# First buffer filled in two loads split by partitions, and the first block's store queued behind the last loads

## The chip, the cores and the metric

One core of a Trainium2 chip. Times are device microseconds (us) of an execution; most executions of one kernel agree within 0.3%. Runs that were repeated are compared in the fast state only.

## The reference, cut to what matters

```
x: 32 x 512 x 1024 float32, random          # 16,384 rows of 1024, 67 MB
return np.sum(x, axis=-1)                   # 16,384 sums
```

## The kernel before

128 partitions hold the rows. A first block gives 112 rows to each partition, a second block 16. A buffer `xt` is 16 rows a partition: 64 KiB in each of 128 partitions, 8 MiB. Three buffers rotate; SyncE issues the loads, VectorE adds up the rows; ScalarE helps with the last two buffers. The very last buffer comes in pieces.

```
while c < whole:
    m = min(G, whole - c)                                    # G = 16 rows
    xt = xpool.tile([P, G * D], F32, tag="xt", name="xt")    # 3 buffers
    parts = (0, 1, m) if done + c == 0 else (0, m)           # first buffer: 1 row, then 15
    for i, k in zip(parts, parts[1:]):
        nc.sync.dma_start(out=xt[:, i * D : k * D], in_=x_b[:, (c + i) * D : (c + k) * D])
    ...                                                      # reductions on VectorE, some on ScalarE
if not final:
    for i, k in ((0, 104), (104, P)):
        nc.scalar.dma_start(out=out_b[i:k], in_=res[i:k])    # first block's sums, 448 B a partition
...                                                          # last loads, in five pieces
store = nc.sync.dma_start(out=out_b, in_=res)                # second block's sums
```

The first two loads are moved ahead of the start-up barrier by a pass over the compiled program, in both kernels.

Of the kernel before, what the change touches and what calls it, by code (L numbers as in the profile page):

```python
# [1 line left out]

# [4 lines left out]

F32 = mybir.dt.float32
ADD = mybir.AluOpType.add
COPY = mybir.ActivationFunctionType.Copy  # L10
X = mybir.AxisListType.X

BLOCKS = (112, 16)
G = 16
ACT_ROWS = 7
CUT = 544
EARLY = 2


@with_exitstack  # L20
def row_sums(
    ctx: ExitStack,
    tc: tile.TileContext,
    x: bass.AP,
    out: bass.AP,
):
    nc = tc.nc
    P = nc.NUM_PARTITIONS

    x_flat = x.flatten_outer_dims()  # L30
    R, D = x_flat.shape
    C = R // P
    assert R % P == 0 and sum(BLOCKS) == C
    out_flat = out.rearrange("a (b c) -> (a b c)", c=1)

    xpool = ctx.enter_context(tc.tile_pool(name="x", bufs=3))
    rpool = ctx.enter_context(tc.tile_pool(name="res", bufs=1))


    tail = rpool.tile([P, D + 16], F32, name="tail")  # L40
    part = tail[:, CUT + 14 : CUT + 15]
    nc.vector.memset(tail[:, CUT + 15 : CUT + 16], 0.0)  # L42
    seen = rpool.tile([P, 2], F32, name="seen")
    pairs = [rpool.tile([P, D // 2], F32, name=f"pairs{i}") for i in range(3)]

    def rows_dve(xt, res, j, n, c):
        nc.vector.tensor_reduce(  # L47
            out=res[:, c : c + n],
            in_=xt[:, j * D : (j + n) * D].rearrange("p (j d) -> p j d", d=D),
            axis=X,  # L50
            op=ADD,
        )

    def sum_act(v, acc):
        return nc.scalar.activation(out=v, in_=v, func=COPY, accum_out=acc)  # L55

    by_act = []

    def rows_act(xt, res, j, n, c):
        for i in range(n):  # L60
            by_act.append(
                sum_act(xt[:, (j + i) * D : (j + i + 1) * D], res[:, c + i : c + i + 1])
            )

    def pairs_dve(v, a, b, acc, pairs):
        h = (a + b) // 2
        nc.vector.tensor_tensor_reduce(  # L67
            out=pairs[:, 0 : h - a], in0=v[:, a:h], in1=v[:, h:b], scale=1.0, scalar=0.0,
            op0=ADD, op1=ADD, accum_out=acc,
        )  # L70

    def block(r0, n):
        x_b = x_flat[r0 : r0 + P * n].rearrange("(p c) d -> p (c d)", p=P)
        out_b = out_flat[r0 : r0 + P * n].rearrange("(p c) -> p c", p=P)
        return x_b, out_b, rpool.tile([P, n], F32, name=f"res{r0}")

    full = C - G
    done = 0
    for b, n in enumerate(BLOCKS):
        x_b, out_b, res = block(done * P, n)  # L80
        final = b == len(BLOCKS) - 1
        whole = n - G if final else n
        c = 0
        while c < whole:
            m = min(G, whole - c)
            xt = xpool.tile([P, G * D], F32, tag="xt", name="xt")
            parts = (0, 1, m) if done + c == 0 else (0, m)
            for i, k in zip(parts, parts[1:]):
                nc.sync.dma_start(
                    out=xt[:, i * D : k * D], in_=x_b[:, (c + i) * D : (c + k) * D]  # L90
                )
            a = ACT_ROWS if done + c + m == full else 0
            rows_dve(xt, res, 0, m - a, c)
            rows_act(xt, res, m - a, a, c + m - a)
            c += m
        if not final:

            for i, k in ((0, 104), (104, P)):
                nc.scalar.dma_start(out=out_b[i:k], in_=res[i:k])
        done += n  # L100

    xt = xpool.tile([P, G * D], F32, tag="xt", name="xt")
    cuts = [0, 9, 13, 15]
    for i, k in zip(cuts, cuts[1:]):
        nc.sync.dma_start(out=xt[:, i * D : k * D], in_=x_b[:, (c + i) * D : (c + k) * D])  # L105
    last = 15 * D
    for i, k, gap in ((0, CUT, 0), (CUT, D, 16)):
        nc.sync.dma_start(
            out=tail[:, i + gap : k + gap],
            in_=x_b[:, c * D + last + i : c * D + last + k],  # L110
        )

    by_act.clear()
    for i, k in zip(cuts[:2], cuts[1:3]):
        h = (k - i) // 2
        rows_dve(xt, res, i, h, c + i)
        rows_act(xt, res, i + h, k - i - h, c + i + h)
    pairs_dve(xt, 13 * D, 14 * D, res[:, c + 13 : c + 14], pairs[2])
    rows_act(xt, res, 14, 1, c + 14)
    pairs_dve(tail, 0, CUT, part, pairs[0])  # L120


    nc.vector.tensor_copy(out=seen, in_=tail[:, CUT + 14 : CUT + 16])  # L123
    pairs_dve(tail, CUT + 14, D + 16, res[:, c + 15 : c + 16], pairs[1])


    tc.keep_in_program_order(nc.sync.keepalive_nop([nc.sync.lower_ap(res[:, c + 14 : c + 15])]))
    store = nc.sync.dma_start(out=out_b, in_=res)
    for i in by_act:
        tc.declare_no_dep(store.ins, i.ins, reason="the wait is in the nop before it")  # L130


def kernel(tc: tile.TileContext, x: bass.AP, out: bass.AP):
    row_sums(tc, x, out)
    tc.close()
    tc.compile()  # L136



    sp = mybir.EngineType.SP  # L140
    fn = tc.nc.m.functions[0]
    entry, body = None, None
    for blk in fn.blocks:
        ops = [i for i in blk.instructions if i.engine == sp]
        if entry is None:
            entry = blk
        elif any(i.opcode == "DMACopy" for i in ops):
            body = blk
            break
    code = list(body.instructions)  # L150
    loads = [i for i in code if i.engine == sp][:EARLY]
    for load in loads:
        assert load.opcode == "DMACopy" and not load.sync_info.on_wait
        code.remove(load)
    body.instructions = code
    code = list(entry.instructions)
    at = next(k for k, i in enumerate(code) if i.engine == sp and i.opcode == "Drain")
    code[at:at] = loads
    entry.instructions = code

# [1 line left out]
_INS = ['x']  # L162
_OUTS = [((32, 512), 'float32')]


# [23 lines left out]
```

## Time and profile before

| | before |
|---|---|
| time, median | 162.14 us (162.09 to 162.2, 3 runs) |
| span in the profile | 160.4 us |
| time from one buffer's reduction to the next | 19.35 us |
| VectorE for one buffer | 17.22 us |
| start of the first reduction | 21.84 us |

The page of the kernel before, its parts 1 and 2: busy time by engine, then what the DMA engines moved in each of 40 equal slices of the span (4.0 us each).

```profile
span 160.4 us, 122 instructions
DVE 121.4 (76%) x17; ACT 17.2 (11%) x31; POOL 0.2 (0%) x4
...
GB/s 376 490 368 368 490 523 261 523 523 261 523 523 261 523 523 261 523 523 261 523 507 278 523 490 294 523 474 310 523 425 359 523 392 392 441 395 369 431 393 79
```

The slices swing between 261 and 523 only because a packet of 64 KiB is counted whole where it starts (16 of them in a slice of 4.01 us make 261 GB/s, 32 make 523). Averaged over three slices the rate is some 435 GB/s (523, 261 and 523 make 436) from shortly after the start to near the end. With VectorE waiting for every buffer, the loads have no slack: a microsecond that the DMA engines lose at the start should be a microsecond at the end.

### The profile page before, as it was taken

Reading aid. Unit: us, or ns where it says so; the run is one execution under the profiler, and the core shown is the slowest. Engines: PE = TensorE matmul, PEld = TensorE weight load, DVE = VectorE, ACT = ScalarE, POOL = GpSimd, SP = SyncE. Lnnn points to the kernel's source line nnn. Section 1 sums busy time; section 2 is a strip of 40 time slices with the busy share of each in tenths; the row PEclk is TensorE's granted clock in tenths of the full one; section 3 lists DMA queues with packets and bytes.
Section 4 is the critical chain, followed back from the end, with each engine's and each line's share of the span. In section 5 each row is a group of like instructions: output and inputs, shape, how many; then the busy total and the mean of one; then the engine's idle time right before and its main releaser. Section 6 shows DMA issues by size and latency. Waiting matters only on the chain.

```text
span 160.4 us, 122 instructions
## 1 busy us (share of the span) xinstructions
DVE 121.4 (76%) x17; ACT 17.2 (11%) x31; POOL 0.2 (0%) x4
## 2 busy tenths in 40 slices
DVE  0000059997799959999499994999949998698883
ACT  0000000000000000000000000000000000695892
POOL 0000000000000000000000000000000000000000
DMA  9988996996996996996996996997998999998992
GB/s 376 490 368 368 490 523 261 523 523 261 523 523 261 523 523 261 523 523 261 523 507 278 523 490 294 523 474 310 523 425 359 523 392 392 441 395 369 431 393 79
DMA packets 2169, 67.18 MB, mean 419 GB/s; under 512 B 505, under 2 KB 633, under 8 KB 889
## 3 DMA queue, kind: packets, MB, share of 16 engines
q1 hardware_dynamic: 2016, 67.12, 97.4%
q10 hardware_dynamic: 153, 0.06, 0.1%
HBM read 67.11 MB, written 0.07 MB: 419 GB/s over the span
## 4 chain that ended last, share of the span: by engine, by line
DMA 75%; DVE 22%; SPq 0%; issue 0%; DVEq 0%
DMA xt<-in_x_dram 75%; DVE res L47 21%; DVE pairs L67 1%; SPq L105 0%; DVE seen L123 0%; DVE tail L67 0%; DVEq L136 0%; DVE res L67 0%
## 5 line engine op out<-in xcount | busy, mean ns | idle before, releaser
L47 DVE TENSOR_REDUCE res<-xt 128x16 f32<-128x16384 f32 (+3 forms) x9 | 119.8, 13308 | 35.1 <-DMA xt<-in_x_dram 35.1
L55 ACT ACT_TABLE_LOAD x1 | 1.3, 1283 | 137.9 <-DMA xt<-in_x_dram 137.9
L55 ACT ACTIVATE xt<-xt 128x1024 f32<-128x1024 f32 x15 | 15.6, 1043 | 2.5 <-DMA xt<-in_x_dram 2.5
L55 ACT ACTIVATION_READ_ACCUMULATOR xt<-xt 128x1 f32 x15 | 2.8, 186 | 0.0
L42 DVE MEMSET tail<- 128x1 f32 x1 | 0.1, 59 | 1.3 <-PEq L173 1.3
L67 DVE CUSTOM_DVE_ANT_0 pairs<-xt 128x512 f32<-128x512 f32 x1 | 0.7, 692 | 0.3 <-DMA xt<-in_x_dram 0.3
L67 DVE CUSTOM_DVE_ANT_0 pairs<-tail 128x272 f32<-128x272 f32 (+1 forms) x2 | 0.9, 426 | 0.0
L123 DVE COPY seen<-tail 128x2 f32<-128x2 f32 x1 | 0.2, 168 | 0.0
L67 DVE DVE_READ_ACCUMULATOR2_ANT res<- 128x1 f32 x2 | 0.2, 82 | 0.0
L173 POOL MEMSET const-bfloat16-1.0<- 128x1 bf16 x1 | 0.1, 103 | 0.0
L173 POOL MEMSET const-uint8-127<- 128x1 uint8 x1 | 0.1, 102 | 0.0
L173 POOL MEMSET const-float32-1.0<- 128x1 f32 x1 | 0.1, 100 | 0.0
L173 POOL MEMSET const-float32-0.0<- 128x1 f32 x1 | 0.1, 99 | 0.2 <-issue 0.2
L67 DVE DVE_READ_ACCUMULATOR2_ANT tail<- 128x1 f32 x1 | 0.1, 80 | 0.0
## 6 DMA issues: line engine op xcount, KB each, us to landing
xt<-in_x_dram SPq DMA_DIRECT2D x1, 7680.0 KB
xt<-in_x_dram SPq DMA_DIRECT2D x1, 4608.0 KB, 32.6
xt<-in_x_dram SPq DMA_DIRECT2D x1, 2048.0 KB, 37.1
xt<-in_x_dram SPq DMA_DIRECT2D x1, 1024.0 KB, 39.2
xt<-in_x_dram SPq DMA_DIRECT2D x1, 512.0 KB, 3.6
tail<-in_x_dram SPq DMA_DIRECT2D x1, 272.0 KB, 39.3
tail<-in_x_dram SPq DMA_DIRECT2D x1, 240.0 KB, 39.2
xt<-in_x_dram SPq DMA_DIRECT2D x6, 40.8
```

Source lines behind the costliest of these rows:

```text
L42: nc.vector.memset(tail[:, CUT + 15 : CUT + 16], 0.0)
L47: nc.vector.tensor_reduce(out=res[:, c : c + n], in_=xt[:, j * D : (j + n) * D].rearrange("p (j d) -> p j d", d=D), axis=X, op=ADD,)
L55: return nc.scalar.activation(out=v, in_=v, func=COPY, accum_out=acc)
L67: nc.vector.tensor_tensor_reduce(out=pairs[:, 0 : h - a], in0=v[:, a:h], in1=v[:, h:b], scale=1.0, scalar=0.0, op0=ADD, op1=ADD, accum_out ...
L123: nc.vector.tensor_copy(out=seen, in_=tail[:, CUT + 14 : CUT + 16])
L173: nc = _bacc.Bacc("TRN2", target_bir_lowering=False, num_devices=1)
```

## The change

Its intent, as far as the code shows it: let the first load be short in descriptors (16 rows of 64 KiB, one for each DMA engine) so that bytes flow early, and keep the first block's store out of the way of the last loads.

```diff
-            parts = (0, 1, m) if done + c == 0 else (0, m)
+            parts = (0, 16, P) if done + c == 0 else (0, P)
             for i, k in zip(parts, parts[1:]):
-                nc.sync.dma_start(
-                    out=xt[:, i * D : k * D], in_=x_b[:, (c + i) * D : (c + k) * D]
-                )
+                nc.sync.dma_start(out=xt[i:k, 0 : m * D], in_=x_b[i:k, c * D : (c + m) * D])
...
         if not final:
-            for i, k in ((0, 104), (104, P)):
-                nc.scalar.dma_start(out=out_b[i:k], in_=res[i:k])
+            out_a, res_a = out_b, res
...                                   # behind the last loads:
+    for i, k in ((0, 64), (64, P)):
+        nc.sync.dma_start(out=out_a[i:k], in_=res_a[i:k])
```

## The prediction

> **What bounds the kernel now.** I read the page first, then the order of time near the start and at the end, then the records of single DMA packets in the trace. Part 3 of the page comes first, because this kernel reads 67 MB and computes little:
>
> ```profile
> DMA packets 2169, 67.18 MB, mean 419 GB/s; under 512 B 505, under 2 KB 633, under 8 KB 889
> ## 3 DMA queue, kind: packets, MB, share of 16 engines
> q1 hardware_dynamic: 2016, 67.12, 97.4%
> q10 hardware_dynamic: 153, 0.06, 0.1%
> ```
>
> The queue of loads keeps all 16 DMA engines busy for 97.4% of the span; hardly anything is left to fill. VectorE, the next busiest, is at 76%. The order of time shows the same from the consumer's side:
>
> ```profile
> 99.18 17.22 DVE L47 TENSOR_REDUCE res<-xt 128x16 f32<-128x16384 f32 x1 [2.14 <-DMA xt<-in_x_dram]
> ...
> 118.53 17.22 DVE L47 TENSOR_REDUCE res<-xt 128x16 f32<-128x16384 f32 x1 [2.13 <-DMA xt<-in_x_dram]
> ...
> 137.88 9.75 DVE L47 TENSOR_REDUCE res<-xt 128x9 f32<-128x9216 f32 x1 [2.13 <-DMA xt<-in_x_dram]
> ```
>
> One 8 MiB buffer arrives every 19.35 us (118.53 - 99.18; again 137.88 - 118.53), 8,388,608 B / 19.35 us = 433.5 GB/s, and VectorE needs 17.22 us for it and then stands idle for 2.13 us until the next lands. Eight such periods are 154.8 us of the 160.4 us span. The chain of waits names VectorE for 21.5%, but only because it follows a buffer's release back to a reduction: the six plain full loads take 40.8 us from issue to landing, two periods, so each stands behind a whole load already queued, and a reduction that ends a little earlier or later changes nothing.
>
> The end, and the store that is moved:
>
> ```profile
> 147.72 0.99 ACTq L99 DMA_DIRECT2D out_dram<-res  x2
> ...
> 156.52 0.69 DVE L67 CUSTOM_DVE_ANT_0 pairs<-xt 128x512 f32<-128x512 f32 x1 [0.28 <-DMA xt<-in_x_dram]
> ...
> 158.18 0.35 SPq L128 DMA_DIRECT2D out_dram<-res  x1
> ```
>
> The first block's store goes out at 147.72 us, 9 us ahead of the last loads; after these land, 1.66 us of VectorE work and the final store remain.
>
> In the packet records, a full load is 128 packets of 65,536 B, 8 on each DMA engine, each taking 2.418 us, that is 27.1 GB/s an engine, one after the other without gaps. The first packets start 1.01 us into the span; after the eight 4,096 B rows of the first load the engines begin their second load between 2.72 and 3.28 us, and this spread stays.
>
> [...]
>
> **The change part by part.** First the small parts.
>
> *The store.* Removed from the middle of the last loads: on one engine up to 8 + 2 packets of 448 B at 25 ns and two semaphore packets of 9 ns, some 0.27 us. They are put behind the last load, 8 packets an engine, 0.2 us, between the last load's packets (157.2 us) and the final store's (159.03 us), so hidden. SyncE has nothing else to do from 118.9 to 157.7 us, so its wait for the first block's results (ready at 147.6 us) holds up no load. Worth: -0.25 us.
>
> *The start.* One packet of 64 KiB on each engine in place of eight of 4 KiB. Eight rows at 0.159 us are 1.27 us, yet the slowest engine took 3.28 - 1.01 = 2.27 us. If long packets ramp without that loss, up to -0.5 us, less than the 1.0 us because the same late starts of engines stay. Descriptors and bytes are otherwise nearly the same in number.
>
> *The first 16 partitions.* 16 rows of 64 KiB, one an engine[...] four rows take 4 x 2.418 = 9.67 us[...]. Unhindered it would be 2.418 us. **Cost: +7.25 us**, on the path, because [...]the queue never has a gap in which to catch up.
>
> *The other 112 partitions.* Seven rows an engine. I take it [...]that the rows are dealt in runs of seven consecutive partitions, engine e getting 16 + 7e and up. [...]
>
> *Sum*, if the ports bind: 162.14 + 7.25 + (5 to 9.7) - 0.75 = 174 to 178 us. Everything after the first buffer shifts as a whole: the next reduction is still released by a load, the next loads are still issued a load ahead, and 19.35 us a buffer cannot be shortened.
>
> **The rivals.** *A: ports do not bind.* Each engine is the limit at 27.1 GB/s and any partition is as good as another. Then 1 + 7 rows are 8 rows as before, and only the small parts remain: 161.4 us. For it: whoever writes such a first split presumably saw it do no harm[...].[...]
>
> *B: only the first load suffers.* [...]just +7 to +10 us is left: 169 to 172 us.
>
> *C: the store becomes the bound.* SyncE sleeps on the first block's results and the final store is late. Against it: those results are there 10 us before the last load lands, and nothing but the nop and the final store follows. Worth at most 0.5 us.
>
> *D: VectorE catches up.* It is idle 2.13 us a buffer, but it has nothing to work on until a load lands, so it recovers none of a late load. Rejected.
>
> **Range and chances.** I give the port mechanism about two in three: [...]nothing in the trace shows it. Within it I expect 168 to 180 us with most weight at 172 to 178; without it 161.4, at most 1 us either way. Prediction 174 us, range 161 to 180 us, which covers both worlds; beyond it lies unfair sharing of ports. Slower by over 2% (above 165.4 us) 0.66; within 2% 0.33; faster by over 2% (under 158.9) 0.01, as 97.4% busy engines leave no such gain.
>
> **What would show it right or wrong.** If right, the first reduction starts near 38 us rather than 21.84, the first 65,536 B packets take about 9.7 us each instead of 2.4, later buffers keep 19.35 us, and the share of busy DMA engines stays high although GB/s is low in the first tenth of the span. If rival A is right, the first reduction starts near 21.5 us with packets of 2.4 us. If B, near 30 us. For the store: semaphore packets of q10 gone, q1 at 160 packets more than the loads' own change, and the last load to the end of the span as before, some 3.2 us from the last reduction's first part. What would make the sum wrong: another dealing of the 112 rows over engines[...].

Its sum came to 174 to 178 us: 162.14, + 7.25 for the first 16 partitions, + 5 to 9.7 for the other 112, - 0.75 for the store and the start. The 7.25 is 3 x 2.418 us; that four rows get the rate of one engine between them was an assumption then, which p1 bears out below (8.8 us a packet). "Port" is whatever engines share that write partitions of one group; the probes below show how such groups behave, not what they are.

## The result, and the profile after

184.24 us (183.97 to 184.35, 4 runs) against 162.12 us: ratio 1.1362, 95% interval 1.1342 to 1.1382, slower. Ratios here are the mean time of one kernel's fast runs over that of the other's of the same rounds, so not quite the ratio of the quoted medians. The direction was foretold; the size was not, for the stated range ended at 180 us.

The page of the changed kernel, the same lines and the queues (slices of 4.6 us):

```profile
span 182.2 us, 123 instructions
DVE 121.5 (67%) x17; ACT 17.1 (9%) x31; POOL 0.2 (0%) x4
...
GB/s 230 29 201 230 403 259 230 230 230 259 446 446 460 460 460 460 417 389 374 432 460 460 460 460 460 389 345 432 446 460 460 460 460 417 323 453 396 409 332 15
...
q1 hardware_dynamic: 2048, 67.18, 96.8%
```

VectorE does the same work to 0.1 us. All the difference is in the first ten slices, some 46 us, in which the loads run at 230 GB/s on average, about half the rate; from the eleventh slice on the rate is as before. Yet the share of busy DMA engines is still 96.8%: a packet that waits counts as busy. A busy DMA engine is thus no proof of a full rate; the GB/s line has to be read beside it.

Order of time of the changed kernel: start us, duration, engine, operation, and in brackets the idle time before it.

```profile
43.92 17.22 DVE L47 TENSOR_REDUCE res<-xt 128x16 f32<-128x16384 f32 x1 [42.53 <-DMA xt<-in_x_dram]
63.20 17.22 DVE L47 TENSOR_REDUCE res<-xt 128x16 f32<-128x16384 f32 x1 [2.05 <-DMA xt<-in_x_dram]
82.54 17.22 DVE L47 TENSOR_REDUCE res<-xt 128x16 f32<-128x16384 f32 x1 [2.13 <-DMA xt<-in_x_dram]
...
169.78 1.16 SPq L113 DMA_DIRECT2D out_dram<-res  x2
...
178.24 0.69 DVE L67 CUSTOM_DVE_ANT_0 pairs<-xt 128x512 f32<-128x512 f32 x1 [0.19 <-DMA xt<-in_x_dram]
...
179.93 0.35 SPq L130 DMA_DIRECT2D out_dram<-res  x1
```

The first reduction starts at 43.92 us in place of 21.84: 22.1 us later, which is the whole loss (184.24 - 162.12 = 22.1). The second follows 19.28 us on, the third 19.34 us after that, the period of before. From the first reduction to the final store's issue it takes 136.0 us here and 136.3 us before.

The trace has a record of every packet. A packet of an engine starts where its last one ended, so the packets can be joined to 16 chains, one for each DMA engine. The mean over the 16 engines of the time of one 64 KiB packet (my sums over those records; two engines whose packets end together can change places in the chains, which leaves the means as they are; the kernel named `e3_one_load` is an experiment below that loads the same buffer in one piece):

```
packet of the engine          1     2     3     4     5     6     7     8   | next buffer's 1st, 2nd
changed kernel, mean us     8.57  5.25  4.67  3.15  4.02  4.50  4.61  4.53 |  3.13  2.42
  (load of)                  16   112   112   112   112   112   112   112
e3_one_load, mean us        3.07  2.42  2.42  2.42  2.42  2.42  2.42  2.42 |  2.42  2.42
```

The first row took 7.6 to 9.3 us on every engine. The seven rows of the 112-partition load took 30.7 us on average (32.5 on the slowest engine) where 16.9 would do.

### The profile page after: what moved, and what is told of

Read it like the earlier page. It is cut to its first block, busy times and chain, and to the rows that moved or that the text cites. A ratio compares the mean times of both kernels' runs of the same rounds, so it can differ in the third digit from the quotient of the medians.

```text
span 182.2 us, 123 instructions
## 1 busy us (share of the span) xinstructions
DVE 121.5 (67%) x17; ACT 17.1 (9%) x31; POOL 0.2 (0%) x4
## 2 busy tenths in 40 slices
DMA packets 2048, 67.18 MB, mean 369 GB/s; under 512 B 512, under 2 KB 640, under 8 KB 768
## 3 DMA queue, kind: packets, MB, share of 16 engines
q1 hardware_dynamic: 2048, 67.18, 96.8%
## 4 chain that ended last, share of the span: by engine, by line
DMA 68%; DVE 29%; another core or an unknown queue 1%; SPq 1%; issue 0%; DVEq 0%
DMA xt<-in_x_dram 68%; DVE res L47 28%; DVE pairs L67 1%; SPq L102 0%; SPq L90 0%; DVE seen L125 0%; DVEq L47 0%; DVE tail L67 0%; DVE res L67 0%; DVEq L138 0%
## 5 line engine op out<-in xcount | busy, mean ns | idle before, releaser
L55 ACT ACTIVATE xt<-xt 128x1024 f32<-128x1024 f32 x15 | 15.6, 1043 | 2.2 <-issue 2.2
```

The lines of the kernel that those rows point to most:

```text
L55: return nc.scalar.activation(out=v, in_=v, func=COPY, accum_out=acc)
```

## The experiments

Theories at the start. **Groups, fair sharing** (the prediction's): engines that write the same group of partitions have the rate of one engine between them, the other engines run at 2.42 us a packet. **Groups, with others held up**: engines that write elsewhere are slowed too. ("Port theories" in the expectations are these two.) **HBM addresses**: rows at a pitch of 448 KiB, read in another pattern by the engines, are slow at the source. **The store**: some of the 22 us is the new place of the store. Differences below are to the runs of before of the same job.

### The two halves of the change apart

`e1_store_only`: the changed kernel with the first buffer loaded as before. `e2_first_only`: the reverse.

```diff
 e1, on the changed kernel            -  parts = (0, 16, P) ...    +  parts = (0, 1, m) ...   (and its load by columns)
 e2, on the kernel before             -  parts = (0, 1, m) ...     +  parts = (0, 16, P) ...  (and its load by partitions)
```

> The change's store alone, with the first buffer loaded as before. If the first buffer's two loads are the whole cost: 161.9 us, within 0.3 us of before (ratio 0.998 to 1.000), first reduction at 21.8 us. If the store behind the loads costs anything of the 22 us (rival): over 165 us.

> The change's first loads of 16 and 112 partitions alone, the store as before. Theory: 184.2 to 184.6 us and a first reduction at 43.9 us, all of the loss. Rival (half from the store): under 180 us.

e1: 162.06 us (5 runs) against 162.1, ratio 0.9996, interval 0.9983 to 1.0008: the same. e2: 183.97 us (4 runs; 0.2 us under what was expected), ratio 1.1344, interval 1.1325 to 1.1362. All of the loss is the first buffer's, and the store as a cause falls. Order of time of e1:

```profile
21.94 17.22 DVE L47 TENSOR_REDUCE res<-xt 128x16 f32<-128x16384 f32 x1 [20.56 <-DMA xt<-in_x_dram]
...
147.79 1.16 SPq L115 DMA_DIRECT2D out_dram<-res  x2
...
158.03 0.35 SPq L132 DMA_DIRECT2D out_dram<-res  x1
```

From the first reduction to the final store's issue: 136.09 us, before 136.34 us. This looks like the quarter of a microsecond foretold, but it is not shown to be the store's: with the store left in its old place the same stretch takes 135.93 us in e2's trace and 136.06 us in e3's (the next experiment). The times, whose interval is 0.2 us to either side, don't resolve it either. The store is issued at 147.79 us as before, by another engine, and holds up nothing.

### The first buffer in one load

```diff
-            parts = (0, 1, m) if done + c == 0 else (0, m)
+            parts = (0, m)
```

> The first buffer in one load of 128 partitions, the store as before. If number and length of packets at the start do not matter[...]: 162.0 to 162.6 us, first reduction near 21.8 us, packets of 2.42 us. Also the base for the probes. A rival that blames long 64 KiB packets at the start: first packets far over 2.4 us and some us of loss.

162.18 us (5 runs), ratio 1.0006, interval 0.9992 to 1.002. Long packets at the start are no trouble, and no gain either: the first packet of each engine takes 3.07 us in place of 2.42, so the start-up loss of some 0.65 us is there with long packets too. My term of up to -0.5 us for it was nothing. This kernel is the base of the probes below.

### The source: the same partitions, other HBM addresses

The block's rows are handed out so that a buffer is one contiguous 8 MiB; a partition's 64 KiB lies right behind its neighbour's, not 448 KiB away. Results are right, as the store's pattern is changed to match.

```diff
-        x_b = x_flat[...].rearrange("(p c) d -> p (c d)", p=P)
+        x_b = x_flat[...].rearrange("(i p j) d -> p i (j d)", p=P, j=G)
```

> As after, but the block's rows are assigned so that a buffer is one contiguous 8 MiB in HBM (rows of 64 KiB one behind the other in place of a pitch of 448 KiB); partitions and their dealing stay. Ports as cause: as slow as after, first reduction near 43.9 us, first packets 7.6 to 9.3 us, the next seven 4.2 to 4.8 us. HBM addresses as cause: first reduction near 21.8 us, or anything clearly other than 43.9.

183.91 us (one look). Its first reduction, in the order of time:

```profile
43.78 17.22 DVE L47 TENSOR_REDUCE res<-xt 128x16 f32<-128x16384 f32 x1 [42.40 <-DMA xt<-in_x_dram]
```

The mean packets are 8.77, 5.38, 4.69, 3.21, 3.79, 4.43, 4.70 and 4.53 us, the changed kernel's within 0.25 us (the seven after the first average 4.4 us), in a quite different region of addresses. The HBM theory falls.

### Probes: one extra load ahead of everything

Each probe puts one extra load of n rows of 64 KiB ahead of e3's loads, into chosen partitions of the third buffer; that buffer's own load overwrites it later, so the result stays right. The HBM rows are the first n partitions' in each, so only the destination varies. I take it that an n-row load gives one row to each of n DMA engines (the extra load of p7, two rows, has two semaphore packets; the 16 loads and stores of the changed kernel, each on 16 engines, have 256) and that the other engines, which have none of it, start at once on the first buffer.

```diff
+    nc.sync.dma_start(out=first[2][0:8, :], in_=x_0[0:8, 0 : G * D])     # p3; others: 0:106:7, 0:29:4, 0:4, ...
```

First, four probes to tell the two group theories apart:

> One load of before (first buffer in one piece) plus one extra load ahead of all, 16 rows of 64 KiB into partitions 0 to 15 of the third buffer (overwritten later, the result stays right).[...] Both port theories: 16 packets of 7.6 to 9.7 us and some +9.7 us of time on e3_one_load; without port limits: 2.4 us packets and +2.4 us.

> The same extra load of the same 16 HBM rows, into partitions 0, 7, 14 to 105[...]. Lock-step theory (all engines go at the pace of the most shared port): all 16 packets near 4.8 us, +4.8 us. Fair sharing of single ports (the prediction): 12 packets of 2.4 us, 4 of 4.8 us. HBM addresses: 8 to 9 us as in p1, for the rows read are the same.

> Extra load of 8 rows into partitions 0 to 7: [...]engines 8 to 15 have no share in it and start at once on the first buffer[...]. Fair sharing: 8 packets near 9 us, the other 8 engines at 2.42 us a packet from the start. Lock-step: the other engines are slowed too, to well over 3 us a packet, for as long as the 8 last.

> As p3 with the same 8 HBM rows, into partitions 0, 4 to 28[...]. Both port theories: no packet much over 2.5 us (first ones apart), +2.4 us on e3_one_load for the engines 0 to 7. If it is the count of partitions and not the ports: 9 us as in p3.

Then, when p3 had shown that engines outside the crowd are held up too, four for the number of engines and groups:

> Extra load of 4 rows into partitions 0 to 3: [...]the other 12 engines start at once on the first buffer[...]. If any hot port slows every engine to its pace: all 16 first packets near 8.4 us, +9 us of time. If it takes more than one hot port, or engines only near it are slowed: the 12 others clearly under 8 us. Fair sharing: the 12 others at about 3 us (first packet of a start), 2.42 us after.

> Extra load of 2 rows into partitions 0 and 1[...]. Any hot port slows all: first packets near 4.8 us everywhere, +4.8 us. Partial coupling: two packets near 4.8 us, the others between 2.8 (start) and 4.8. Row 4 of the changed kernel[...] had 2 packets near 4.7 us and 14 near 2.9 us, so partial coupling is what I expect here.

> Extra load of 4 rows into partitions 0, 2, 4 and 6[...]. If the number of hot ports decides: the 12 others are slowed to 4.8 us here and not in p7. If only the load of the hottest port decides: as p7.

> Extra load of 3 rows into partitions 0 to 2[...]. Three packets near 7.3 us either way. If three engines held up are enough to hold up all: the 13 others near 6.5 to 7 us. If it takes four, as p6 and p8 had: the 13 others near 3 us, as in p7.

What was measured. A group here is four neighbouring partitions, 0 to 3, 4 to 7 and so on to 28 to 31, as far as these probes show it: one row in each of eight groups took 3.05 us a packet (p4), four rows in one 8.5 us (p6), eight rows in two 8.3 us (p3), four rows in two 4.5 us (p8). "Crowded" engines share one. The packets of the extra load are the first n to start; only in p7 the starts don't part so clearly, and I name the two long packets of the 16 (the two semaphore packets of its extra load, at 5.96 and 6.06 us, agree with their ends).

| probe | partitions | groups x engines on each | crowded engines | first packet, engines of the extra load (median) | first packet, the other engines (median) | time against before |
|---|---|---|---|---|---|---|
| p4 | 0, 4 to 28 | 8 x 1 | 0 | 3.05 us | 2.85 us | 165.08, +3.0 us |
| p7 | 0, 1 | 1 x 2 | 2 | 5.16 and one near 4.3 us | 3.0 us | 166.61, +4.4 us |
| p9 | 0 to 2 | 1 x 3 | 3 | 6.6 us | 3.0 us | 168.52, +6.6 us |
| p8 | 0, 2, 4, 6 | 2 x 2 | 4 | 4.5 us | **4.4 us** | 167.04, +4.8 us |
| p6 | 0 to 3 | 1 x 4 | 4 | 8.5 us | **8.5 us** | 171.14, +8.9 us |
| p3 | 0 to 7 | 2 x 4 | 8 | 8.3 us | **8.4 us** | 171.03, +8.9 us |
| p2 | 0, 7 to 105 | 16 x 1 | 4, by their times | 4.1 us | (none) | 167.36, +5.2 us |
| p1 | 0 to 15 | 4 x 4 | 16 | 8.8 us | (none) | 171.40, +9.3 us |

The first reduction in p7 and then in p6, one line of the order of time each, and below it the stretch from 2 to 8 us (last two figures: DMA share and GB/s):

```profile
26.40 17.22 DVE L47 TENSOR_REDUCE res<-xt 128x16 f32<-128x16384 f32 x1 [25.12 <-DMA xt<-in_x_dram]
...
2.00:8.00 6.00, 0.00 (x0) 0.00 (x0) 0.00 (x0) 1.00 0.77 328
```

```profile
30.90 17.22 DVE L47 TENSOR_REDUCE res<-xt 128x16 f32<-128x16384 f32 x1 [29.59 <-DMA xt<-in_x_dram]
...
2.00:8.00 6.00, 0.00 (x0) 0.00 (x0) 0.00 (x0) 1.00 0.54 66
```

A packet is counted where it starts: in these 6 us 30 packets of 64 KiB start in p7, but 6 in p6, where the twelve engines without a row of the extra load are stuck as well.

Three things follow. (1) It is which partitions are written and not how many: 8 rows cost 3.0 us in 8 groups (p4) and 8.9 us in 2 (p3), from the same HBM rows. (2) Engines on one group have about the rate of one between them: two, three and four engines took about 5, 6.6 and 8.5 us for a packet of 2.42 us; the four rows of p6 took 9.2 us together, 28 GB/s, where one engine alone moves 27.1. (3) With two engines held up, the others run freely: 3.0 us, as at any start, and 2.42 us for the next packet. With three, nearly so: 3.0 us, but 3.0 us again for the next packet (p9). **With four or more held up, all sixteen are slowed, in p3, p6 and p8 to the pace of the crowded ones** (others 8.4, 8.5 and 4.4 us), though twelve (p6, p8) or eight (p3) of them have no row of the extra load. My expectation for p8 left open whether groups or engines count; p6 and p8 together say that four held-up engines suffice, on one group or on two.

Fair sharing therefore falls. In p2 the four longest first packets were 4.7 to 5.5 us, as for two pairs that meet, though no two of its partitions are in one group of four: so partitions farther apart seem to meet as well; which, no run tells. Fair sharing would have left the other twelve near 3 us; they took 3.5 to 4.3 us (median of all 16: 4.1 us), with the next packet at about 3.4 us in place of 2.42. Nor is it lock-step to the letter, which would have given 4.8 us on all 16.

What it is that the engines share, and why four held-up engines suffice, is not shown.

### How the 112 rows are dealt out, and another split

The sum took it that an engine gets seven consecutive partitions. `e6_by_sevens` deals them so by construction, as seven loads of 16 rows (taking it that a load of 16 rows gives one row to each engine in turn).

```diff
+   rows = [slice(0, 16)] + [slice(16 + j, 16 + j + 7 * 15 + 1, 7) for j in range(7)]     # first buffer
+   for r in rows:
+       nc.sync.dma_start(out=xt[r, 0 : m * D], in_=x_b[r, c * D : (c + m) * D])
```

> As after, but the 112 rows come as seven loads of 16 rows at a step of seven partitions (16, 23, 30 to 121, then 17 and so on), so that each engine gets by construction what I assumed for the one load of 112: seven consecutive partitions. If the assumption holds: the same mean packets row by row as after (5.3, 4.7, 3.2, 4.0, 4.5, 4.6, 4.5 us after the first), first reduction near 43.9 us, time within 1 us of 184.2. If the load of 112 is dealt otherwise: another sequence of packet times.

183.95 us, first reduction at 43.84 us, and the packets row by row 8.50, 5.32, 4.71, 3.24, 3.97, 4.60, 4.67, 4.48 us against the changed kernel's 8.57, 5.25, 4.67, 3.15, 4.02, 4.50, 4.61, 4.53. The pattern is the same to 0.1 us, down to the odd fourth packet: there two engines took 4.6 to 4.9 us and the other 14 about 3 us, in both kernels. So the dealing in sevens agrees with the one load of 112. Two long packets and the rest near 3 us is also what p7 shows for one pair. The 4.0 us of the fifth row I have not worked out.

`e5_halves`: first loads of 64 and 64 partitions.

```diff
-            parts = (0, 16, P) if done + c == 0 else (0, P)
+            parts = (0, 64, P) if done + c == 0 else (0, P)
```

> As after, with first loads of 64 and 64 partitions in place of 16 and 112. [...]8 rows at 2 x 2.418 us are 38.7 us in place of 19.3, so first reduction at 41 us (21.8 + 19.3) or 1 to 2 us earlier, time 180 to 181.5 us. If small first loads or 16 partitions are the trouble rather than ports: near 162 us.

183.49 us against 162.25 us for the kernel before (one look each), 21.2 us for one 8 MiB buffer; first reduction at 43.59 us. That is 2 us slower than I expected: my expectation took it that in each half every engine meets one other at every row, and a packet took 5.12 us in place of 2 x 2.42 = 4.84, on all engines and in nearly all rows, so 6% beyond the halving; why, I have not tested. 16 x 65,536 B / 5.12 us = 205 GB/s. Which partitions of a half meet, no run tells.

No version here beats the kernel before by more than the noise; e1 is level with it.

## Why the prediction was right or wrong, point by point

- *What bounds the kernel*: right. A loss of 22.1 us at the first buffer was a loss of 22.1 us at the end, and nothing was caught up. Rival D, rejected, is shown wrong by the unchanged period.
- *The first 16 partitions, +7.25 us*: right in mechanism and nearly in size. The same load alone cost 9.3 us in p1, which is 6.9 us beyond the 2.4 us of its bytes; in the changed kernel it was 6.0 us (see the sum). Rival A (any partition is as good as another), to which I gave a third, is wrong: 8 rows cost 3.0 us in p4 and 8.9 us in p3.
- *The other 112 partitions, "(5 to 9.7)"*: **this is the term that failed.** Its working, an estimate with fair sharing over a layout that no run shows, is cut. Measured: 30.7 us on average and 32.5 us on the slowest engine where 16.9 would do, so +13.8 to +15.6 us in place of at most +9.7. The assumed dealing in sevens agrees with e6, to 0.1 us row by row. Fair sharing is what the probes contradict: in p8, with two pairs that meet, the other engines took 4.4 us in place of 3. Five of the seven rows here took 4.50 to 5.25 us a packet, near 2 x 2.42 = 4.84 and on all engines alike (4.2 to 5.8 us); the fourth took 3.15 us and the fifth 4.02; together 30.7 us. That these five rows are p8's case is my reading; the trace does not name the partition of a packet. I also let the figure fall from 9.7 towards 5; it went the other way. Rival B, which let this term go to nearly nothing, is wrong by more.
- *Sum*. Read from the last of the 16 engines to end: the first row ended at 10.86 us (4.90 in e3), the eighth at 43.19 us (21.80). That is 6.0 us for the first row and 15.4 us for the other seven, 21.4 of the 22.1 us. Of the rest, 0.3 us is e3's first reduction against before's (22.16 and 21.84 us) and 0.4 us lies between the last packet and the reduction (0.73 against 0.36 us in e3).
- *The start, -0.5 us*: wrong, nothing was gained (e3, ratio 1.0006). *The store, -0.25 us*: not shown. The trace of e1 is 0.25 us shorter behind the first reduction than that of before, but so are those of e2 and e3, which have the old store, and the times cannot tell it from nothing. Rival C is wrong: the final store was not late.
- *Signs named beforehand*: first packets about 9.7 us (7.6 to 9.3), later buffers 19.35 us apart, a high busy share at low GB/s (for a quarter of the span, not a tenth), and the packets of the moved store (2016 - 128 for the loads + 160 = 2048 on q1): all seen. First reduction near 38 us: 43.92, by the term that failed.

## What to carry to other kernels

Where loads bound a kernel as here, split a transfer along the columns and keep all 128 partitions in each piece: before's split by columns and one whole load cost the same, every split by partitions tried here cost over 20 us. When a load touches few partitions, count how many of its rows fall into one group of four neighbours, and expect that with four or more engines held up, as in these probes, the whole set of engines, and with it every load queued behind, is slowed to about that pace (p6: 8.5 us a packet on all, the first reduction at 30.90 us in place of 22.16). And read the GB/s line beside the DMA engines' busy share, for a waiting packet looks busy.
